# Moving two of sixteen expert weight buffers into the place of layer 1's operands, and re-cutting the others as 10, 2 and 2

## The chip, the core and the metric

The kernel runs on one core of a Trainium2 chip. The metric is the device time of one execution in microseconds, lower is better. The core has a matrix engine (PE, with its weight loads shown as PEld), two engines for element-wise work (DVE and ACT), a general one (POOL) and SP, which in this kernel issues nearly all DMAs. All DMAs that SP issues stand in one queue in order: a DMA whose wait isn't over holds back those behind it.

## The reference, cut to what matters

Two layers of a diffusion backbone over 256 latent and 256 context tokens, width 1024. Each layer has a mixer (an mLSTM head group and an attention head group) and a channel mixer. The second layer's channel mixer is a mixture of 8 experts, of which each latent token uses 2:

```
h = modulate(rms(x));  p = h @ w_in;  y = mixer(p)
x = x + gate1 * (y @ w_out)
layer 0: x = x + gate2 * swiglu(modulate(rms(x)))            # dense
layer 1: top2 = top_k(h @ router, 2)                           # latent tokens alone
         x = x + gate2 * sum_e w_e * (silu(h @ wg[e]) * (h @ wu[e])) @ wd[e]
return rms(x)
```

All is in float32. An expert has three matrices of 1024 x 3584, so the 8 experts bring 352 MB of weights in, and each is read once.

## The kernel before, in words

Up to the experts the kernel works on activations that are kept transposed, features on partitions and 512 tokens in the columns. The operand of every large product is held as a high and a low part (`hh0` to `hh7` and `hl0` to `hl7`, 16 tiles of 128 x 512, made at L319 and listed in `hp`). `gemm` (L342) runs over 128-column units of a weight stream: `Stream` loads a piece (`raw`, L140), ACT and DVE split it into `wh` and `wl` (L149, L150), and three matmuls (L335 to L337) make one product. `mixer` (L388) runs the input projection (`projections`, L766) woven with the mLSTM heads, the attention and the modulation products `adas` (L234), whose weights come as `araw` (L206), two buffers for each step. When the last unit of the input projection is done, the finished heads are written back into `hp` by `split` (L551), in layer 1 into its latent columns 256 to 511 alone. `project` (L796) multiplies them with `w_out`.

The expert weights are taken in the order in which the experts use them: for each expert 2 halves of 8 gate tiles (`in_mg`) and 8 up tiles (`in_mu`) of 896 KB, and then 14 down tiles (`in_md`) of 1024 KB, 46 tiles for an expert and 368 in all. `Ahead` (L931) is their loader. It keeps a ring of `sum(NRW)` = 16 buffers `rawe` of 8 KB a partition. `issue(upto)` issues loads until `upto` of them are out, and `done(left)` issues the next ones for the buffers that the products have just given back. So tile number 16 goes to the buffer of tile 0 and waits for the matmuls that read tile 0.

The ring stands in two pools. `RW` (L929) has 8 buffers and lies where the mixer's tiles lay, so it opens when the mixer of layer 1 is over. `RX` (L1014) has 8 and lies where the weight stream's tiles and `hp` lay (the pools `PW` and `PA`), so it opens when the last product of `project` has read them. `loader.issue(NRW[0])` at L970 issues the first 8 loads and `loader.issue(sum(NRW))` at L1015 the other 8.

Behind `project` come the router (logits L1004, ranks L1081 to L1085), the gathering of the first expert's tokens (L1115) and `experts` (L1159). There the tokens of an expert stand in groups of 32 (`GROUPS`): two groups always, a third behind a branch (L1169) if the expert has more than 64 tokens. `up` (L1177) is run for gate and up, in two steps of 4 tiles each (`UPS`), each step over all groups, so 4 buffers come free only when the last group of a step is done with them. `down` is like it with its own steps (`DOWNS`); L1185 is the up matmul and L1215 the down matmul. `turn` (L1231) transposes the hidden values (`hT`, L1237). A scheduler orders the instructions of each engine when the kernel is built.

Of the kernel before, what the change touches and what calls it, by code (L numbers as in the profile page):

```python
# [9 lines left out]
F32 = mybir.dt.float32  # L10
F32R = mybir.dt.float32r
# [8 lines left out]
KT = 8  # L20
TOK = 512
CTX = 256
# [20 lines left out]
SC = 448  # L43

STEPS = (((0, 1, 56, 30), (7.5, 3.2, 2.2, 4.6)), ((0, 1, 45, 20), (6, 2.2, 2.2, 4.6)))
NRW = (8, 8)


UNITS = ["g", "k0", "k1", "q0", "q1", "v0", "v1", "v2", "v3",
# [6 lines left out]
TAILD = 3  # L56
# [18 lines left out]
def tile_hybrid(ctx: ExitStack, tc, a, tap=None):  # L75
# [23 lines left out]
    def run(g):  # L99
        for _ in g:  # L100
            pass

    def step(g, n=1):
        for _ in range(n):
            next(g, None)

    def upto(g, mark):
        for m in g:
            if m == mark:
                return  # L110


    p1, pa, pw = ExitStack(), ExitStack(), ExitStack()
    P1 = p1.enter_context(tc.tile_pool(name="p1", bufs=1, side="right", reuse_waits="tile"))
    PA = pa.enter_context(tc.tile_pool(name="pa", bufs=1, side="right", reuse_waits="tile"))
    PW = pw.enter_context(tc.tile_pool(name="pw", bufs=1, side="right", reuse_waits="tile"))
# [14 lines left out]
    class Stream:  # L131


        def __init__(self, src):
            self.src, self.raw, self.w, self.ahead = src, [], [], 0
# [112 lines left out]
    def mod(layer, i, j):  # L248

        return mods[layer, i // 2][:, (i % 2) * 8:(i % 2) * 8 + 8, j]  # L250
# [10 lines left out]
    def new_acc():  # L261
        return P1.tile([128, TOK], F32, tag="acc", name="acc", bufs=1)
# [45 lines left out]
    def coef(layer, which):  # L308
        w = (n1, n2)[which]
        A = new_coef()  # L310
        for j in range(2):
            if which and layer == 1 and j == 1:
                continue
            dve.scalar_tensor_tensor(A[:, :, j], mod(layer, 3 * which + 1, j), 1.0, w[:, layer, :],
                                     op0=ALU.add, op1=ALU.mult)
        return A


    hp = [(PW.tile([128, TOK], F32R, name=f"hh{k}"), PW.tile([128, TOK], F32R, name=f"hl{k}")) for k in range(KT)]  # L319

    def modulated(A, b, layer, which, halves, ks=range(KT)):

# [18 lines left out]
    def gemm(units, rhs, evac, nk, head=0, halves=False, tail=0):  # L341

        units = list(units)
        n = len(units)
        b0 = base[0]
        base[0] += n * nk
        o = {}

        def product(u, k, c0, c1):
            lo = max(units[u][0], c0)
            if lo >= c1:
                return
            i = k * head + u if u < head else u * nk + k
            wh, wl = stream.tile(b0 + i)
            mm3(o[u][:, lo:c1], wh, wl, rhs[k][0][:, lo:c1], rhs[k][1][:, lo:c1], k == 0, k == nk - 1)

        cuts = [c[:2] for c in HALVES]
        if head:  # L360
            for u in range(head):
                o[u] = ps("mm", name="mm")
            for c0, c1 in cuts if halves else [(0, TOK)]:
                for k in range(nk):
                    for u in range(head):
                        product(u, k, c0, c1)
                        if k == nk - 1 and c1 == TOK:
                            evac(units[u][1], o[u], units[u][0], c1)
                    yield
        for u in range(head, n - tail):  # L370
            o[u] = ps("mm", name="mm")
            for k in range(nk):
                product(u, k, 0, TOK)
            evac(units[u][1], o[u], units[u][0], TOK)
            yield
        if tail:
            yield "tail"
            for u in range(n - tail, n):
                o[u] = ps("mm", name="mm")
            for c0, c1 in cuts:  # L380
                for u in range(n - tail, n):
                    for k in range(nk):
                        product(u, k, c0, c1)
                    evac(units[u][1], o[u], c0, c1)
                    yield


    def mixer(layer, pool, extra):  # L388


        full = layer == 0
# [3 lines left out]
        def units(keys):  # L395
            for k in keys:
                yield q0 if k[0] in "qo" or k in ("a0", "a1", "a2", "a3") else 0, k
# [23 lines left out]
        for h in range(4):  # L421
            z = 64 * (1 - h % 2)
            nc.gpsimd.memset(kz[h][z:z + 64, :], 0.0)
        for h in range(2):
            z = 64 * (1 - h)
# [7 lines left out]
        def flush():  # L433
            while pend:
                f, key = pend.pop(0)
                f()
                ready.add(key)
# [328 lines left out]
        def projections(keys):  # L766

            yield from gemm(units(keys), hp, evac, KT)
            flush()
            done.append(True)  # L770

        def at():
            while not set(qa_keys) <= ready:
                yield
            yield from qk_norm()
            for j in range(4):
                yield from attend(j)
# [24 lines left out]
    def bridge(p, tail, acc, layer, which, g):  # L802

        upto(p, "tail")
        A = coef(layer, which)
        S = Stats(acc[0])
        nxt = base[0] // 8
        step(p, tail)
        stream.ensure(nxt)
        step(p)  # L810
        S.sums(0, CTX)
        stream.ensure(nxt + 1)
        step(p)
        b = S.spread(0, CTX)
        modulated(A, b, layer, which, HALVES[:1], range(0, 3))
        run(p)
        stream.ensure(nxt + 2)
        modulated(A, b, layer, which, HALVES[:1], range(3, 6))
        step(g, 3)
        S.sums(CTX, TOK)  # L820
        modulated(A, b, layer, which, HALVES[:1], range(6, 8))
        step(g, 3)
        S.spread(CTX, TOK)
        modulated(A, b, layer, which, HALVES[1:], range(0, 4))
        step(g, 2)
        modulated(A, b, layer, which, HALVES[1:], range(4, 8))
# [37 lines left out]
    a0, mx = ExitStack(), ExitStack()  # L864
# [22 lines left out]
    S.sums(0, TOK)  # L887
    M0 = mixer_pool("mix0", a0)
    g = mixer(0, M0, adas(lambda: mx.pool, (0, 1), (0, 2), (1, 0)))
    A = new_coef()  # L890
    def products0(k):
        o = ps("ax", name="ada")
        products(o, k, 0, True, True)
        return o

    z = products0(0)
    b = S.spread(0, TOK)
    stream.ensure(0)
    for k in range(KT):
        row = z  # L900
        if k + 1 < KT:
            z = products0(k + 1)
# [15 lines left out]
    p = project(0, 0, acc)  # L918
    acc2 = []
    g = ffn(acc2)  # L920
    bridge(p, TAIL, acc, 0, 1, g)

    p, g = g, mixer(1, mixer_pool("mix1"), adas(lambda: mx.pool, (1, 1), (1, 2)))
    bridge(p, TAILD, acc2, 1, 0, g)
    run(g)
    mx.close()


    RW = ctx.enter_context(tc.tile_pool(name="rw", bufs=1, reuse_waits="tile"))  # L929

    class Ahead:  # L931

# [8 lines left out]
        def issue(self, upto):  # L941
            while len(self.t) < min(upto, len(self.src)):
                i = len(self.t) % sum(NRW)
                pool, n = (RW, NRW[0]) if i < NRW[0] else (RX, NRW[1])
                t = pool.tile([128, 2048], F32, tag="raw", name="rawe", bufs=n)
                src, c = self.src[len(self.t)]
                nc.sync.dma_start(t[:, 0:c], src())
                self.t.append(t)
# [7 lines left out]
        def done(self, left):  # L956

            self.issue(self.n - left + sum(NRW))

    def weights(e):  # L960

        return (lambda w, st, k: a[("mg", "mu")[w]][bass.ds(e(), 1), st, k].squeeze(0),
                lambda c: a["md"][bass.ds(e(), 1), c].squeeze(0))


    turn_of = []
    loader = Ahead([weights(lambda: 0)] + [weights(lambda p=p: turn_of[p - 1]) for p in range(1, NE)])
    acc = [new_acc()]
    p = project(1, CTX, acc)
    loader.issue(NRW[0])  # L970
    wr0 = P1.tile([128, KT, NE], F32, name="wr0")
    nc.gpsimd.dma_start(wr0, a["router"])
    step(p, HEAD)

    g2 = RW.tile([128, D], F32, name="g2")
    g2c = mod(1, 5, 0)
    for c in range(2):
        o = ps("ax", name="g2p")
        for q in range(4):
            k = 4 * c + q  # L980
            pe.matmul(o[:, q * 128:(q + 1) * 128], g2c[:, k:k + 1].to_broadcast([128, 128]), ident,
                      start=True, stop=True)
        act.activation(g2[:, c * 512:(c + 1) * 512], o, AF.Copy)
    zb = RW.tile([128, 512], BF, name="zb")
    nc.gpsimd.memset(zb, 0.0)


    scale, shift = (RW.tile([128, KT], F32, name=n) for n in ("scale", "shift"))
    dve.scalar_tensor_tensor(scale, mod(1, 4, 0), 1.0, n2[:, 1, :], op0=ALU.add, op1=ALU.mult)
# [5 lines left out]
    for k in range(KT):  # L995
        pe.matmul(o[:, 0:NE], shift[:, k:k + 1].to_broadcast([128, 128]), wr0[:, k, :], start=(k == 0), stop=(k == KT - 1))
    lc = RW.tile([128, NE], F32, name="lc")
    act.activation(lc, o[:, 0:NE], AF.Copy)
# [15 lines left out]
    RX = ctx.enter_context(tc.tile_pool(name="rx", bufs=1, reuse_waits="tile"))  # L1014
    loader.issue(sum(NRW))  # L1015
    RS = ctx.enter_context(tc.tile_pool(name="rs", bufs=1, reuse_waits="tile"))
# [23 lines left out]
    with tc.issue_after(behind_lg):  # L1040
        for t in range(2):
            for c in range(2):
                s = slice(c * 512, (c + 1) * 512)
                p = ps("ax", name="xT")
# [260 lines left out]
    with tc.issue_after(behind_oh[0]), tc.issue_after(behind_th):  # L1305
# [4 lines left out]
        rows = lambda v: v.unsqueeze(1).to_broadcast([128, NE, NE])  # L1310
        cols = lambda v: v.unsqueeze(2).to_broadcast([128, NE, NE])
# [211 lines left out]
```

## Time and profile before

| what | us |
|---|---|
| median of 3 runs (lowest, highest) | 1774.93 (1770.13, 1779.02) |
| the profiled execution, its own time | 1775.88 |
| its span in the profile | 1774.1 |
| PE busy in the span | 1713.3 (97%) |
| DVE busy, ACT busy | 600.1, 448.6 |

The profile's span begins with the first instruction and ends with the last one; the execution's own time has 1.8 us around it. Read in 40 slices, PE is busy at nine tenths or more in nearly all of them at the full granted clock. The DMA engines are at two to eight tenths in the first 20 slices; from slice 22 on they move about 419 GB/s, with lower slices of 406, 391 and 338 GB/s (26 to 28) and 160 GB/s in the last.

### The profile page before, as it was taken

To read this page: it belongs to the slowest core of one execution; us is meant where nothing else is said; L and a number is where in the kernel's file an instruction comes from. 1 tells how busy PE (TensorE), PEld (TensorE's weight loads), DVE (VectorE), ACT (ScalarE), POOL (GpSimd) and SP (SyncE) were. 2 spreads that over 40 slices of the span, in tenths; PEclk is the share of its full clock that TensorE was granted. 3 is DMA by queue.
4 is the path that set the end of the run, shared out by engine and by line. 5 is a ranking of instruction groups with operands and counts; after the bars stand their busy time and mean duration, and the time that the engine had idled before them with its cause. 6 is when DMAs were issued, how large, how long until landed. Compare 5 with 4: busy or idle time off the path is not lost. (4 is left out here: it accounts for less than half of the span.)

```text
span 1774.1 us, 31022 instructions
## 1 busy us (share of the span) xinstructions
PE 1713.3 (97%) x13032; PEld 997.4 (56%) x13032; DVE 600.1 (34%) x1400; ACT 448.6 (25%) x863; POOL 19.4 (1%) x42
## 2 busy tenths in 40 slices
PE   6999999999999999998999999999999999999995
PEld 4865457988888889875764433433333343333432
DVE  6734665733333336647531200201212021210213
ACT  4543553422223323545430100100100010100101
POOL 1000000000000000000000000000000000000000
PEclk9999999999999999999999999999999999999997
DMA  8435552232332222365589999998999999999993
GB/s 323 154 107 190 174 180 63 84 95 97 97 104 95 96 96 95 119 198 188 190 357 418 419 419 419 406 391 338 417 419 418 419 404 418 419 418 420 416 418 160
DMA packets 84860, 472.68 MB, mean 266 GB/s; under 512 B 9424, under 2 KB 9808, under 8 KB 69088
## 3 DMA queue, kind: packets, MB, share of 16 engines
q1 hardware_dynamic: 84240, 469.36, 68.0%
q8 instruction: 117, 1.92, 0.4%
q0 software_dynamic: 176, 0.56, 0.1%
q10 hardware_dynamic: 288, 0.52, 0.1%
q14 instruction: 39, 0.32, 0.0%
HBM read 469.36 MB, written 1.05 MB: 265 GB/s over the span
## 5 line engine op out<-in xcount | busy, mean ns | idle before, releaser
L1185 PE MATMUL up<-rawe,G 128*32 128x448 f32 x5120 | 507.2, 540 | 3.7 <-PEq L1169 2.6
L1185 PEld LDWEIGHTS up<-rawe,G 128*32 128x32 f32 x5120 | 184.3, 110 | 301.0 <-issue 280.4
L335 PE MATMUL mm<-hh,wh 128*128 128x512 f32 (+1 forms) x856 | 305.5, 360 | 3.4 <-ACT hh L330 3.4
L336 PE MATMUL mm<-hl,wh 128*128 128x512 f32 (+1 forms) x856 | 304.5, 356 | 0.0
L337 PE MATMUL mm<-hh,wl 128*128 128x512 f32 (+1 forms) x856 | 303.5, 355 | 0.0
L1215 PE MATMUL y<-rawe,e 128*32 128x512 f32 x2240 | 263.7, 593 | 1.8 <-PEq L1169 1.2
L149 ACT ACTIVATE wh<-raw 128x1024 fp32r<-128x1024 f32 x120 | 127.1, 1059 | 326.3 <-PE mm L336 290.7
L150 DVE TENSOR_TENSOR wl<-raw,wh 128x1024 fp32r<-128x1024 f32 x120 | 146.7, 1223 | 176.4 <-ACT wh L149 173.8
L335 PEld LDWEIGHTS mm<-hh,wh 128*128 128x128 f32 x856 | 161.0, 189 | 30.8 <-issue 4.8
L336 PEld LDWEIGHTS mm<-hl,wh 128*128 128x128 f32 x856 | 161.8, 189 | 27.3 <-issue 5.2
L337 PEld LDWEIGHTS mm<-hh,wl 128*128 128x128 f32 x856 | 161.7, 189 | 23.6 <-issue 1.6
L1215 PEld LDWEIGHTS y<-rawe,e 128*32 128x32 f32 x2240 | 78.3, 110 | 160.9 <-issue 155.4
L1238 ACT ACTIVATE e<-hT 128x384 f32<-128x384 f32 x48 | 22.7, 491 | 418.6 <-PE hT L1237 418.6
L1257 DVE TENSOR_TENSOR hid<-sg,up 128x448 f32<-128x448 f32 x48 | 27.0, 617 | 241.8 <-PE up L1185 241.8
L335 PE MATMUL mm<-fh,wh 128*128 128x512 f32 (+1 forms) x209 | 74.5, 356 | 0.0
L336 PE MATMUL mm<-fl,wh 128*128 128x512 f32 (+1 forms) x209 | 74.3, 355 | 0.0
L337 PE MATMUL mm<-fh,wl 128*128 128x512 f32 (+1 forms) x209 | 74.3, 355 | 0.0
L1239 DVE COPY e<-hT 64x128 f32<-64x128 f32 x48 | 13.6, 284 | 163.3 <-ACT e L1238 163.2
L214 PE MATMUL ada<-araw,cz 128*32 128x256 f32 x640 | 54.3, 390 | 13.4 <-DMA araw<-in_ada_dram 13.4
L1154 DVE SCALAR_TENSOR_TENSOR xt<-scat,wet,xt 128x512 f32<-128x512 f32 x32 | 22.6, 746 | 117.4 <-PE scat L1153 117.3
L1140 DVE TENSOR_TENSOR ye<-y,yc 32x512 f32<-32x512 f32 x48 | 32.7, 682 | 73.9 <-ACT yc L1138 73.2
L1253 ACT ACTIVATE sg<-up 128x448 f32<-128x448 f32 x48 | 22.9, 544 | 124.0 <-PE up L1185 124.0
(292 smaller groups left out, 1389.9 us busy)
## 6 DMA issues: line engine op xcount, KB each, us to landing
rawe<-in_mg_dram SPq DMA_DIRECT2D x128, 896.0 KB, 17.4
rawe<-in_mu_dram SPq DMA_DIRECT2D x128, 896.0 KB, 16.2
rawe<-in_md_dram SPq DMA_DIRECT2D x112, 1024.0 KB, 19.1
raw<-in_ws_dram SPq DMA_DIRECT2D x120, 512.0 KB, 3.5
araw<-in_ada_dram SPq DMA_DIRECT2D x80, 512.0 KB, 4.6
a<-in_ada_dram SPq DMA_DIRECT2D x8, 1024.0 KB, 11.2
xall<-in_xT_dram SPq DMA_DIRECT2D x2, 1024.0 KB, 6.3
fn<-in_fn_dram POOLq DMA_DIRECT2D x1, 512.0 KB, 8.8
```

The source lines that it names most:

```text
L149: act.activation(h, raw, AF.Copy)
L150: dve.tensor_sub(l, raw, h)
L214: pe.matmul(o[32 * g:32 * g + 32, 0:256], cz[:, kt, 16 - 2 * row:48 - 2 * row], t[:, z:z + 256], start=(first and kt < 4), stop=(last and ...
L335: pe.matmul(out, wh, hh, start=first, stop=False)
L336: pe.matmul(out, wh, hl, start=False, stop=False)
L337: pe.matmul(out, wl, hh, start=False, stop=last)
L1140: dve.tensor_add(ye[32 * s:32 * s + 32, n * 512:(n + 1) * 512], y[s][32 * n:32 * n + 32, :], yc[32 * n:32 * n + 32, :])
L1185: last = pe.matmul(o[s][32 * c:32 * c + 32, 0:SC], g[:, k, 32 * s:32 * s + 32], w[k][:, c * SC:(c + 1) * SC], start=(k == 0), stop=(k == K ...
L1215: last = pe.matmul(y[s][r:r + 32, :], e[s][:, 2 * i + par, :], w[i][:, par * 1024 + n * 512:par * 1024 + (n + 1) * 512], start=(i == 0), s ...
L1238: act.activation(e[s][:, 12 * st:12 * st + 12, :], pt[:, 0:384].rearrange("p (q c) -> p q c", c=32), AF.Copy)
L1253: act.activation(sg[s], o[:, 0:SC], AF.Silu)
L1257: dve.tensor_mul(hid[st, s], sg[s], o[:, 0:SC])
```

## The change

The tuple of ring sizes becomes four numbers. The 16 operand tiles become four of 8 KB a partition, `hp0` to `hp3`, in a pool `PH` of their own that stays open to the end. In layer 1, when the input projection is done, `hp` is rebuilt from two tiles of the latent columns alone (`hp0` and `hp1` again, read through `Late`, which shifts the columns), and the places of `hp2` and `hp3` take expert tiles 0 and 1, whose loads are issued there. Expert tiles 2 to 11 stand in the mixer's place, 12 and 13 in the places of `hp0` and `hp1` when `project` has read them, 14 and 15 in the weight stream's place. The ring still has 16 buffers.

```diff
-NRW = (8, 8)
+NRW = (2, 10, 2, 2)
+    PH = ctx.enter_context(tc.tile_pool(name="ph", bufs=1, side="right", reuse_waits="tile"))
...
-    hp = [(PW.tile([128, TOK], F32R, name=f"hh{k}"), PW.tile([128, TOK], F32R, name=f"hl{k}")) for k in range(KT)]
+    def parts(n, cols):
+        per = 2048 // cols
+        z = [PH.tile([128, per, cols], F32R, tag=f"hp{i}", name=f"hp{i}", bufs=1) for i in range(n)]
+        z = [z[i // per][:, i % per, :] for i in range(2 * KT)]
+        return list(zip(z[0::2], z[1::2]))
+    class Late:
+        def __init__(self, t):
+            self.t = t
+        def __getitem__(self, at):
+            rows, cols = at
+            return self.t[rows, cols.start - CTX:TOK - CTX if cols.stop is None else cols.stop - CTX]
+    hp = parts(4, TOK)
...
             yield from gemm(units(keys), hp, evac, KT)
             flush()
             done.append(True)
+            if not full:
+                hp[:] = [tuple(Late(z) for z in y) for y in parts(2, CTX)]
+                loader.issue(NRW[0])
...
-                pool, n = (RW, NRW[0]) if i < NRW[0] else (RX, NRW[1])
-                t = pool.tile([128, 2048], F32, tag="raw", name="rawe", bufs=n)
+                pool, tag, n = [(lambda: PH, "hp2", 1), (lambda: PH, "hp3", 1), *[(lambda: RW, "raw", NRW[1])] * NRW[1], (lambda: PH, "hp0", 1),
+                                (lambda: PH, "hp1", 1), *[(lambda: RX, "raw", NRW[3])] * NRW[3]][i]
+                t = pool().tile([128, 2048], F32, tag=tag, name="rawe", bufs=n)
...
-    loader.issue(NRW[0])
+    loader.issue(NRW[0] + NRW[1])
```

The loader itself is now made ahead of layer 1's mixer, since it issues from inside it. Two places in SP's queue move, and one on PE.

In SP's queue between layer 1's mixer and the routing, the order before is this (`raw` is the stream's weights, `araw` the modulation's, `rawe` an expert tile, `number` the experts' order):

```order
L206 DMA araw<-in_ada_dram 128x1024 x4
L140 DMA raw<-in_ws_dram 128x1024
L206 DMA araw<-in_ada_dram 128x1024 x12
L140 DMA raw<-in_ws_dram 128x1024
L947 DMA rawe<-in_mg_dram 128x1792 x8
L947 DMA rawe<-in_mu_dram 128x1792 x5
L1169 UNCONDITIONAL_BRANCH x2
L947 DMA rawe<-in_mu_dram 128x1792 x3
L1351 TENSOR_LOAD number
```

and the same stretch of the changed kernel, whose lines have moved down by 3 to 26:

```order
L209 DMA araw<-in_ada_dram 128x1024 x2
L967 DMA rawe<-in_mg_dram 128x1792 x2
L209 DMA araw<-in_ada_dram 128x1024 x2
L143 DMA raw<-in_ws_dram 128x1024
L209 DMA araw<-in_ada_dram 128x1024 x12
L143 DMA raw<-in_ws_dram 128x1024
L967 DMA rawe<-in_mg_dram 128x1792 x6
L967 DMA rawe<-in_mu_dram 128x1792 x7
L1195 UNCONDITIONAL_BRANCH x2
L967 DMA rawe<-in_mu_dram 128x1792
L1377 TENSOR_LOAD number
```

Two of the sixteen first loads now stand in the middle of a run of four `araw` loads; the other fourteen follow the last `raw` as the sixteen did before.

On PE the instructions and their waits are the same up to the second half of the first expert. There the order before is this (`hT` is a transpose of hidden values, `up` a matmul of an expert tile, the branch guards the third group):

```order
L1185 MATMUL up<-rawe,G 32x448 x27
L1237 MATMUL hT<-sml,hid 128x128 x3
L1237 MATMUL hT<-sml,hid 64x128
L1237 MATMUL hT<-sml,hid 128x128 x3
L1237 MATMUL hT<-sml,hid 64x128
L1185 MATMUL up<-rawe,G 32x448
L1237 MATMUL hT<-sml,hid 128x128 x3
L1237 MATMUL hT<-sml,hid 64x128
L1185 MATMUL up<-rawe,G 32x448 x20
L1169 COMPARE_AND_BRANCH
L1185 MATMUL up<-rawe,G 32x448 x16
L1169 UNCONDITIONAL_BRANCH x2
```

and in the changed kernel this:

```order
L1211 MATMUL up<-rawe,G 32x448 x31
L1263 MATMUL hT<-sml,hid 128x128 x3
L1263 MATMUL hT<-sml,hid 64x128
L1195 COMPARE_AND_BRANCH
L1211 MATMUL up<-rawe,G 32x448 x16
L1195 UNCONDITIONAL_BRANCH x2
L1263 MATMUL hT<-sml,hid 128x128 x3
L1263 MATMUL hT<-sml,hid 64x128
L1211 MATMUL up<-rawe,G 32x448
L1263 MATMUL hT<-sml,hid 128x128 x3
L1263 MATMUL hT<-sml,hid 64x128
L1211 MATMUL up<-rawe,G 32x448 x43
```

The branch with its 16 matmuls has moved from behind the three groups of transposes to between the first and the second. The number of matmuls is the same.

## Rows read from the trace of the kernel before

**Rows 1.** Busy time by stretch: engines (instructions), granted clock, DMA share, GB/s.

```profile
874.00:896.00 22.00, 22.00 (x187) 20.51 (x186) 8.14 (x17) 6.05 (x12) 0.53 (x1) 1.00 0.97 391
896.00:900.00 4.00, 4.00 (x37) 3.58 (x35) 1.24 (x3) 0.42 (x1) 0.00 (x0) 1.00 0.12 48
900.00:915.00 15.00, 14.23 (x108) 9.01 (x105) 11.48 (x68) 10.25 (x18) 0.58 (x1) 1.00 0.95 372
915.00:918.00 3.00, 2.79 (x33) 0.98 (x29) 1.07 (x8) 0.32 (x1) 0.00 (x0) 1.00 1.01 419
1200.00:1240.00 40.00, 40.00 (x352) 15.32 (x348) 4.03 (x13) 3.15 (x7) 0.00 (x0) 1.00 0.82 333
1700.00:1741.00 41.00, 40.34 (x375) 14.25 (x377) 3.39 (x9) 4.25 (x9) 0.00 (x0) 1.00 1.01 418
1741.00:1750.00 9.00, 8.38 (x74) 3.18 (x66) 0.15 (x1) 0.59 (x1) 0.00 (x0) 1.00 0.36 147
```

**Rows 2.** SP's issues in order of time, 850 to 1130 us: start, length, what.

```profile
874.30 4.00 SPq L947 DMA_DIRECT2D rawe<-in_mg_dram  x8
879.82 23.34 SPq L947 DMA_DIRECT2D rawe<-in_mu_dram  x8
918.23 8.80 SPq L947 DMA_DIRECT2D rawe<-in_mg_dram  x8
```

**Rows 3.** SP's waits from 882 to 925 us: total, times, longest.

```profile
SPq L947 <- PE mm L337: 12.6, 1, 12.6
SPq L947 <- PE up L1185: 7.7, 6, 3.4
```

**Rows 4.** PE in order of time, 895 to 935 us.

```profile
899.56 1.26 PE L1004 MATMUL lg<-xall,wr 128*32 128x256 f32 x8
...
912.41 1.31 PE L1185 MATMUL up<-rawe,G 128*32 128x448 f32 x9
...
915.74 10.73 PE L1185 MATMUL up<-rawe,G 128*32 128x448 f32 x112 [0.20 <-PEq L1169]
```

**Rows 5.** Waits of PEld and PE from 912 us on for expert tiles.

```profile
PEld up L1185 <- DMA rawe<-in_mg_dram: 3.2, 7, 1.0
PEld up L1185 <- DMA rawe<-in_mu_dram: 3.1, 8, 0.9
PE up L1185 <- DMA rawe<-in_mu_dram: 0.6, 2, 0.4
PE up L1185 <- DMA rawe<-in_mg_dram: 0.2, 1, 0.2
```

**Rows 6.** SP's waits from 1200 to 1240 us.

```profile
SPq L947 <- PE y L1215: 33.9, 10, 10.6
```

**Rows 7.** DMA issues: count, size of each, median us to landing.

```profile
rawe<-in_mg_dram SPq DMA_DIRECT2D x128, 896.0 KB, 17.4
raw<-in_ws_dram SPq DMA_DIRECT2D x120, 512.0 KB, 3.5
araw<-in_ada_dram SPq DMA_DIRECT2D x80, 512.0 KB, 4.6
```

**Rows 8.** SP's issues around the end of layer 1's input projection.

```profile
810.76 0.33 SPq L206 DMA_DIRECT2D araw<-in_ada_dram  x1
...
819.88 1.73 SPq L206 DMA_DIRECT2D araw<-in_ada_dram  x2
```

**Rows 9.** PE there: the projection's last matmul, the next modulation products.

```profile
811.23 0.28 PE L337 MATMUL mm<-hh,wl 128*128 128x256 f32 x1
...
819.18 1.07 PE L214 MATMUL ada<-araw,cz 128*32 128x256 f32 x16
```

**Rows 10.** Busy time by stretch there, columns as in the first group.

```profile
812.00:815.00 3.00, 3.00 (x13) 1.84 (x13) 2.71 (x7) 2.99 (x8) 0.82 (x2) 1.00 0.46 168
815.00:820.00 5.00, 4.20 (x32) 2.42 (x30) 4.66 (x16) 2.93 (x8) 1.23 (x2) 1.00 0.01 2
```

**Rows 11.** PEld in the first expert's transposes, idle before each in brackets.

```profile
945.19 0.83 PEld L1237 LDWEIGHTS hT<-sml,hid 128*128 128x128 f32 x8 [0.73 <-issue]
...
947.09 0.39 PEld L1237 LDWEIGHTS hT<-sml,hid 128*128 128x128 f32 x4 [0.73 <-DVE e L1239]
```

More of the change, by code (lines that the diff above doesn't have):

```diff
@@ L923, in tile_hybrid @@
     p, g = g, mixer(1, mixer_pool("mix1"), adas(lambda: mx.pool, (1, 1), (1, 2)))
[L924 to L929, printed above, removed]
     class Ahead:
@@ L967, in tile_hybrid @@
     loader = Ahead([weights(lambda: 0)] + [weights(lambda p=p: turn_of[p - 1]) for p in range(1, NE)])
+    bridge(p, TAILD, acc2, 1, 0, g)
+    run(g)
+    mx.close()
+    RW = ctx.enter_context(tc.tile_pool(name="rw", bufs=1, reuse_waits="tile"))
     acc = [new_acc()]
     p = project(1, CTX, acc)
-    loader.issue(NRW[0])
+    loader.issue(NRW[0] + NRW[1])
     wr0 = P1.tile([128, KT, NE], F32, name="wr0")
```

## The prediction, made before the changed kernel ran

> **What bounds the kernel now.** I read the stretches first, then SP's queue, since the change moves only DMAs, and then PE around the moment at which the experts start.
>
> The experts take almost half of the span. In the stretches the reader is to see two things full at once: PE is busy in nearly all of each stretch, and the DMA engines move 418 or 419 GB/s in the steady ones [rows 1]. Both can't be the limit everywhere, so I ask who waits for whom. From the first expert matmul at 912.41 us [rows 4] PE's matmuls and weight loads wait for expert tiles for 3.2 + 3.1 + 0.6 + 0.2 = 7.1 us in all, no wait longer than 1.0 us [rows 5]. The pace agrees: 112 up matmuls in 10.73 us [rows 4] are 0.38 us for four that run side by side, with no gap between fours. SP on its side waits for PE: from 1200 to 1240 us 33.9 us go into waiting for down products to give buffers back [rows 6], and the DMA share falls to 0.82 there [rows 1]; all 16 buffers are full and the DMA engines have nowhere to write. So PE's chain of expert products from 912.41 us sets the end, and the DMA engines keep up with it with about 7 us lost.
>
> Ahead of the experts the DMA engines do have holes: after 9 tiles (8 loads at 874.30 us and one at 879.82 us [rows 2]) SP waits 12.6 us for the last matmuls of the output projection [rows 3], and from 896 to 900 us only 48 GB/s move [rows 1]. The other seven tiles follow up to 903.2 us (879.82 + 23.34) [rows 2]. The change fills that hole and another one in the mixer. What it is worth depends on what happens at 918.23 us, where the 17th load is issued [rows 2]: the queue waits there for PE's up matmuls, 7.7 us over six waits, the longest 3.4 [rows 3], because that load goes to the buffer of tile 0, which is in use until both groups have passed the first four tiles.
>
> **The change part by part.**
>
> *Two loads earlier, at the end of layer 1's input projection.* A tile is 896 KB [rows 7], 0.918 MB, and takes 0.918 / 0.419 = 2.19 us at the steady rate; two take 4.4 us. They wait for the projection's last matmul, at 811.23 + 0.28 = 811.5 us [rows 9], and stand behind the `araw` load issued at 810.76 us [rows 8], which is 0.52 MB or 1.25 us. So they are in at about 817.5 us. The `araw` loads behind them wait for the products that start at 819.18 us and are issued at 819.88 us [rows 8, 9]; from 815 to 820 us the DMA engines are idle, share 0.01 [rows 10]. That idle time is the cover: cost 0, with 2.4 us to spare. Without it an `araw` pair would come up to 4.4 us late, and PE with it. Below zero there is nothing, as no work waits for the pair before 912 us. I take 0.
>
> *Ten loads instead of eight when the mixer's place comes free.* Same issue time, 874.30 us, and the same wait ahead of it. With the last `raw` piece (0.52 MB) they are 9.70 MB, 23.1 us, and keep the engines full up to about 898 us. No `raw` piece is left to be delayed; the one beside them is first in the queue. Cost on the path 0.
>
> *Four loads instead of seven behind the projection.* From about 899.6 us, when the matmuls give way to the logits [rows 4], four tiles take 8.8 us and are in at 908.4 us. Before, seven took 15.3 us and were in by about 918 us, with 419 GB/s still moving from 915 to 918 us [rows 1]. So the sixteenth tile lands 9.6 us earlier.
>
> *What this is worth.* The start of the experts doesn't need it. Between 899.56 us and 912.41 us PE runs the routing and the gathering of tokens [rows 4], and these depend on no expert tile. The first expert's gate tiles are 0 to 7, in since 896 us both ways; its first up tile is wanted after 8 gate tiles in two groups, 16 steps of two fours of 0.38 us each, 12 us after the start, at 924 us, when all 16 tiles are in both ways. The 17th load still waits for PE at 918.23 us. So from 918 us on the two kernels are in the same state: 16 tiles landed, none in flight, the same ring of 16 and the same order. What the change gains is turned into a longer idle time of the DMA engines, 908 to 918 us. Bounds: 0 on one side; on the other 7.1 us, all of PE's waits for expert tiles [rows 5], if every one of them came from a ring that was late from the start. The stall at 1200 us speaks for 0: there the ring is full, so whatever lead the loads had is cut off. I take 0.
>
> *Operands in four tiles, and the latent halves in two.* The matmuls, splits and modulations keep their number, shape, order and, on PE, their waits up to the middle of the first expert; one split in layer 1 waits for four more matmuls of the projection, at most 4 x 0.28 us [rows 9], off PE's path. Cost 0, bounds 0 and 1.1 us.
>
> *The order in the first expert.* The branch moves in between the transposes. Around these PEld has two gaps of 0.73 us [rows 11]; one branch or matmul more in between can close them or add one of the same size, so the bounds are -1.5 and +1.5 us. As one branch and three groups stand there both ways, I take 0.
>
> **The sum.** The profiled execution took 1775.88 us, 1774.1 us of span and 1.8 us around it. With 0 for every part the changed kernel's like is 1775.9 us. That profile lies 0.95 us above the median of the three runs, 1774.93 us, so the median to expect is 1774.9 us.
>
> The page "DMA: Bandwidth & Descriptors" of the Trainium skill (Rules for kernel authors) advises to issue a DMA early, compute, and wait on it late; read as a promise for this change it gives the first rival below. No run here has shown it yet, and the row at 918.23 us speaks against it, because the early loads don't make the next one early.
>
> **The rivals.**
>
> *The early loads carry through (faster).* If the ring's lead at 918 us counted, up to 9.6 us of loading would be saved, of which PE could use its 7.1 us of waits: 1774.9 - 7.1 = 1767.8 us. For it: the DMA engines are full in nearly every stretch from 900 to 1741 us [rows 1]. Against it: SP waits for PE at 918.23 us [rows 3], and again at 1200 us [rows 6]. It decides only if the 17th load no longer had to wait for PE, and the ring is not longer than it was. Chance 0.06.
>
> *The early pair blocks the modulation's weights (slower).* SP's queue holds fourteen `araw` loads behind the pair. If the pair were issued later than about 815.5 us (819.88 - 4.4), because the last reader of its place is later than the matmul at 811.23 us, the next `araw` pair would land up to 4.4 us late, PE would wait at its modulation products, and mixer, projection and experts would all follow: 1774.9 + 4.4 = 1779.3 us. For it: PE runs these products as soon as it comes to them, and the place of the pair lies in the order in front of them. Against it: 8 us between the last reader and the next `araw` issue [rows 8, 9]. Chance 0.06.
>
> The same page of the Trainium skill (Queues, rings and completion order) says that descriptors on one engine's ring are consumed in ring order; by that the full 4.4 us would fall on the `araw` loads and not a share of it. The rows here show no such case.
>
> *The early loads aren't early (no change).* If the pair waited for something else of the mixer it would land with the ten at 874 us. Twelve tiles from 874.30 us and four from 899.6 us would then be in at about 910 us, still ahead of 918.23 us. The time is the same, so this shares the forecast's 0.88 with the case that all goes as computed.
>
> **How the numbers follow.** 0.88 for no effect, at 1774.9 us; 0.06 for 1767.8 us; 0.06 for 1779.3 us. The three runs before lie from 1770.1 to 1779.0 us, so a median of the changed kernel may lie some 4 us to either side without any cause. About 0.5%, 8.9 us, is what a measurement of this kernel can tell from no change. Both rivals are smaller than that (-0.4% and +0.25%), so most of their chance falls to "same" too; they pass the bound only together with that scatter. That gives 0.06 faster, 0.89 same, 0.05 slower. For 8 times in 10 the range must hold the scatter and reach to both rivals: 1768 to 1781 us.
>
> **What would show it right or wrong.** In the changed profile two `in_mg` loads are issued at about 811.6 us and the next modulation products start at 819.2 us as before. The stretch 896 to 900 us is full, the one from 909 to 918 us is empty. The first expert matmul stands at 912.4 us and the 17th load at 918.2 us. The dip between 1200 and 1240 us is still there, and the last expert matmul ends at about 1750 us, as in [rows 1]. It is wrong if the first expert matmul moves by more than 2 us, if the modulation products wait for `araw` after 819 us, or if the experts take another time from first to last matmul at the same start.

## The result, and the profile after

The changed kernel takes 1784.89 us (median of 8 runs, 1783.86 to 1790.37) against 1776.12 for the kernel before (8 runs); the ratio is 1.0057, with a 95% interval of 1.0047 to 1.0067. I had forecast no effect and a time up to 1781; it is slower, and by more than my 0.5%. The profiled execution took 1784.85 us, 8.97 more than that of before.

The loads are issued in the forecast order. SP's issues in order of time, of the changed kernel, in answer to [rows 2, 8] (start, length, what):

```profile
819.43 0.90 SPq L967 DMA_DIRECT2D rawe<-in_mg_dram  x2
...
881.85 4.45 SPq L967 DMA_DIRECT2D rawe<-in_mg_dram  x6
886.34 22.30 SPq L967 DMA_DIRECT2D rawe<-in_mu_dram  x8
925.59 9.05 SPq L967 DMA_DIRECT2D rawe<-in_mg_dram  x8
```

and PE in order of time, in answer to [rows 4]:

```profile
906.93 1.27 PE L1030 MATMUL lg<-xall,wr 128*32 128x256 f32 x8
...
919.76 1.31 PE L1211 MATMUL up<-rawe,G 128*32 128x448 f32 x9
...
923.09 10.73 PE L1211 MATMUL up<-rawe,G 128*32 128x448 f32 x112 [0.21 <-PEq L1195]
```

The pair goes out early, and the 17th load goes out 5.83 us after the first expert matmul, as before (918.23 - 912.41 = 5.82). But that matmul comes at 919.76 us and not at 912.41, and everything here is 7.35 us late. Busy time by stretch, columns as in [rows 1], each stretch of before moved by 7.35 us:

```profile
881.35:903.35 22.00, 22.00 (x188) 20.51 (x187) 7.91 (x18) 6.05 (x12) 0.00 (x0) 1.00 0.96 390
903.35:907.35 4.00, 4.00 (x37) 3.59 (x35) 1.22 (x3) 0.42 (x1) 0.00 (x0) 1.00 0.89 321
907.35:922.35 15.00, 14.19 (x107) 9.01 (x105) 11.47 (x68) 10.23 (x18) 0.58 (x1) 1.00 0.70 272
922.35:925.35 3.00, 2.79 (x33) 0.97 (x29) 1.07 (x8) 0.32 (x1) 0.00 (x0) 1.00 0.00 0
1207.35:1247.35 40.00, 40.00 (x352) 15.31 (x348) 4.01 (x13) 3.14 (x7) 0.00 (x0) 1.00 0.84 336
```

The hole between projection and logits is filled (DMA share 0.89 for 0.12), the idle time has moved to just ahead of the 17th load (0.00 for 1.01), PE does the same work in the same time in each stretch, and the dip at 1200 us is still there. So the loss lies ahead of all this. The page's groups of matmuls show it. Of the kernel before (busy us, mean ns of one, behind the bar):

```profile
L335 PE MATMUL mm<-hh,wh 128*128 128x512 f32 (+1 forms) x856 | 305.5, 360 | 3.4 <-ACT hh L330 3.4
L336 PE MATMUL mm<-hl,wh 128*128 128x512 f32 (+1 forms) x856 | 304.5, 356 | 0.0
L337 PE MATMUL mm<-hh,wl 128*128 128x512 f32 (+1 forms) x856 | 303.5, 355 | 0.0
```

and of the changed kernel:

```profile
L355 PE MATMUL mm<-hp,wh 128*128 128x512 f32 (+1 forms) x856 | 308.7, 364 | 4.2 <-ACT hp L350 4.0
L356 PE MATMUL mm<-hp,wh 128*128 128x512 f32 (+1 forms) x856 | 307.7, 360 | 0.1
L357 PE MATMUL mm<-hp,wl 128*128 128x512 f32 (+1 forms) x856 | 306.6, 359 | 0.0
...
L355 PE MATMUL mm<-fh,wh 128*128 128x512 f32 (+1 forms) x209 | 74.5, 356 | 0.0
```

The same 2568 matmuls on these operands (`hh` and `hl` before, `hp` after) are 4 ns longer in the mean, with 0.9 us more waiting in all; those on the feed-forward operand `fh` keep the 356 ns that they have before. Matmuls overlap in the pipeline, so what one costs is the step from start to start. Two stretches full of `mm` matmuls give it, the first on `hp`, the second on `fh` and `fl`. All such stretches from here on count only the instructions that write or read `mm`, on DVE and ACT too. The kernel before (columns: PE, PEld, DVE, ACT, granted clock, DMA share, GB/s):

```profile
400.00:450.00 50.00, 50.00 (x222) 41.42 (x221) 2.77 (x4) 2.91 (x5) 1.00 0.31 99
475.00:515.00 40.00, 40.00 (x178) 33.14 (x177) 5.20 (x12) 0.00 (x0) 1.00 0.31 100
```

and the changed kernel:

```profile
400.00:450.00 50.00, 50.00 (x215) 40.18 (x214) 3.46 (x5) 2.31 (x4) 1.00 0.29 93
475.00:515.00 40.00, 40.00 (x178) 33.10 (x178) 5.24 (x12) 0.00 (x0) 1.00 0.29 94
```

PE is busy for all 50 us in both, at the full granted clock, and yet it starts 222 matmuls in one and 215 in the other. By their start times a 512-column matmul on `hp` takes 226.7 ns before in the steady stretches and 234.3 after; on `fh` it takes 227 in both. Up to the end of layer 0's feed-forward layer, 1485 of them follow each other without a wait, at a mean of 227.4 and 234.2 ns: 10.2 us. 277 matmuls of 256 columns are 1.3 ns shorter: -0.4 us. That is 9.8, and the next matmul there stands at 692.51 us before and 702.35 after: 9.84. Some 2.5 us come back in layer 1, so that PE is 7.35 us late at the experts: between these two points PE waits 5.5 us in all for the modulation's weights (`araw`) before and 2.8 us after. This wait is no fixed size: in a later run with the pace of before (the kernel before with a plain ring) PE waits 3.3 us there and the first expert matmul comes at 909.88 us. So the 7.35 us hold some 2 us of scatter, and the sum over the matmuls, 9.8 us, is the better measure of what the change costs. 1.63 us are lost again at the end, and 7.35 + 1.63 = 8.98 is the whole difference.

The last 1.63 us stand at the last down products. PE in order of time, of the kernel before:

```profile
1741.49 6.06 PE L1215 MATMUL y<-rawe,e 128*32 128x512 f32 x50
1748.09 1.92 PE L1215 MATMUL y<-rawe,e 128*32 128x512 f32 x16 [0.54 <-SPq L1360]
```

and of the changed one:

```profile
1749.68 4.38 PE L1241 MATMUL y<-rawe,e 128*32 128x512 f32 x36
1754.61 1.92 PE L1241 MATMUL y<-rawe,e 128*32 128x512 f32 x16 [0.56 <-SPq L1386]
1757.08 1.92 PE L1241 MATMUL y<-rawe,e 128*32 128x512 f32 x16 [0.54 <-SPq L1386]
```

It breaks off twice, because the last tiles come later. The first and the last expert matmul are 837.01 us apart before and 838.64 after.

### The profile page after: what moved, and what is told of

It is laid out like the page before. It is cut to its first block, busy times and chain, and to the rows that moved or that the text cites. A ratio compares the mean times of both kernels' runs of the same rounds, so it can differ in the third digit from the quotient of the medians.

```text
span 1783.1 us, 31032 instructions
## 1 busy us (share of the span) xinstructions
PE 1722.6 (97%) x13031; PEld 993.7 (56%) x13032; DVE 600.3 (34%) x1400; ACT 448.4 (25%) x863; POOL 19.3 (1%) x42
## 5 line engine op out<-in xcount | busy, mean ns | idle before, releaser
L355 PE MATMUL mm<-hp,wh 128*128 128x512 f32 (+1 forms) x856 | 308.7, 364 | 4.2 <-ACT hp L350 4.0
L356 PE MATMUL mm<-hp,wh 128*128 128x512 f32 (+1 forms) x856 | 307.7, 360 | 0.1
L357 PE MATMUL mm<-hp,wl 128*128 128x512 f32 (+1 forms) x856 | 306.6, 359 | 0.0
L355 PEld LDWEIGHTS mm<-hp,wh 128*128 128x128 f32 x856 | 160.6, 189 | 35.0 <-ACT hp L350 5.4
L356 PEld LDWEIGHTS mm<-hp,wh 128*128 128x128 f32 x856 | 161.4, 189 | 30.6 <-issue 5.2
L357 PEld LDWEIGHTS mm<-hp,wl 128*128 128x128 f32 x856 | 161.3, 188 | 26.9 <-issue 1.6
```

Source lines behind the costliest of these rows:

```text
L355: pe.matmul(out, wh, hh, start=first, stop=False)
L356: pe.matmul(out, wh, hl, start=False, stop=False)
L357: pe.matmul(out, wl, hh, start=False, stop=last)
```

## The experiments

**What could change the pace of a matmul that is itself unchanged.** The change moves the operands in the on-chip memory: in the built programs `hh0` begins at byte 105536 of a partition and `hp0` at 196576, the weights `wh` at 146496 and 113728, `fh` at 18240 in both. My first theories were A, that the start of the moving operand must be a multiple of 64 bytes, whatever the weights' is; C, that the place high in the memory is slow; and B, that the early loads cost the time.

*The changed kernel with operands on a multiple of 64 bytes.*

```diff
+    pad0 = PH.tile([128, 8], F32, name="pad0")
     hp = parts(4, TOK)
+    pad1 = PH.tile([128, 8], F32, name="pad1")
```

> The changed kernel with 32 bytes of padding ahead of the operand tiles hp0 to hp3 and 32 behind them, so that they start at byte 196544 of a partition (a multiple of 64) instead of 196576 (32 past one); all else keeps its place modulo 64. Theory A (a 512-column matmul whose moving operand starts 32 bytes past a multiple of 64 takes 234 ns from start to start instead of 227): back to the kernel before, 1774 to 1779 us, 227 ns, first expert matmul at 912 to 913 us. Theory B (the two early loads cost the time): still 1783 to 1787 us. Theory C (the place at the end of the partition costs it, whatever its alignment): still 1783 to 1787 us and 234 ns.

Measured: 1781.34 us, ratio 1.0034 (1.0022 to 1.0046). The stretches of above:

```profile
400.00:450.00 50.00, 50.00 (x216) 40.41 (x215) 3.46 (x5) 2.32 (x4) 1.00 0.30 94
475.00:515.00 40.00, 40.00 (x177) 32.86 (x176) 5.25 (x12) 0.00 (x0) 1.00 0.31 95
```

Still 216 and not 222: A falls. (B and C had 1783 to 1787 us, which the median misses too.) `fh`, which has not moved, is slower too (229 ns), and what has moved against it are the weights, by 64 bytes.

*The kernel before with operands moved by 32 bytes, weights not; and with the weights moved by 32 and the operands by 64.*

```diff
+    pad0 = PW.tile([128, 8], F32, name="pad0")     # both; ahead of hp in the first, behind it in the second
     hp = [(PW.tile([128, TOK], F32R, name=f"hh{k}"), PW.tile([128, TOK], F32R, name=f"hl{k}")) for k in range(KT)]
+    pad1 = PW.tile([128, 8], F32, name="pad1")     # behind hp in the first, behind late_consts() in the second
```

> The kernel before with its 16 operand tiles 32 bytes past a multiple of 64 (hh0 at byte 105504 instead of 105536), every other tile where it was modulo 64. Theory A: as slow as the changed kernel up to the experts, +6 to +9 us, 1782 to 1786 us, 234 ns for 512 columns. Theories B and C: as before, 1774 to 1779 us, 227 ns.

> The kernel before with the weight stream's tiles raw, wh and wl 32 bytes past a multiple of 64 and the operands hh, hl on one. Theory A (only the moving operand counts, since a weight load lies beside the matmul ahead of it): no change, 1774 to 1779 us. A rival of it (any operand of a matmul off a multiple of 64 costs): +6 to +13 us.

Measured: ratios 1.0051 (1.0034 to 1.0067) and 1.0057 (1.0039 to 1.0076). So the kernel before becomes nearly as slow as the changed one by a pad of 32 bytes (233.3 ns for 234.3), with its operands at the low place and without early loads: C isn't needed, nor is B. A had forecast this first result; for the second it had forecast no change, and it fails again. In the second run the matmuls on `fh` become slower as well, though `fh` stands where it stood:

```profile
400.00:450.00 50.00, 50.00 (x216) 40.25 (x216) 3.46 (x5) 2.33 (x4) 1.00 0.30 95
475.00:515.00 40.00, 40.00 (x173) 32.15 (x172) 4.38 (x10) 0.00 (x0) 1.00 0.33 97
```

*The changed kernel without the early call of the loader.* `loader.issue(NRW[0])` was taken out of the mixer.

> The changed kernel without the two early issues: tiles 0 and 1 are issued with the ten at the end of the mixer, all places in memory as in the changed kernel. Theory A: as slow as the changed kernel, 1783 to 1787 us, since the operands lie where they lay. Theory B: back to 1774 to 1779 us.

Measured: 1.0067 (1.0048 to 1.0087). This experiment failed: the scheduler still puts the two loads in front of the modulation's, and SP issues them at 819.10 us. It repeats the changed kernel and says nothing on B; the last run below does.

**The difference between the two places.** Theory R: what counts is the start of the moving operand less that of the weights, modulo 128 or 256 bytes. It is 0 in the kernel before and 160 in the changed one. (In the three expectations that follow, B is another theory, that both starts count by themselves.) First the cost by itself:

```diff
+    for n, step in ((2, 1), (1, 27)):
+        for c in range(64):
+            m, w = divmod(c * step % 64, 8)
+            for cols in (512, 256):
+                for _ in range(n):
+                    group(8 * m, 8 * w, cols)
```

> This kernel computes nothing of the reference: it runs only chains of 24 float32r matmuls like those of the projections and the feed-forward layer (eight steps of three: weight 1 on operand 1, weight 1 on operand 2, weight 2 on operand 1), 512 and 256 columns wide, with no DMA beside them. The start of the moving operand goes through the eight multiples of 32 bytes within 256, and that of the weights too: 64 pairs, each visited twice in different orders, with 48 and then 24 matmuls of each width; the output is zeros. Theory R (relative): a 512-column matmul takes 226.7 ns from start to start where the moving operand and the weights have the same offset modulo 128 or 256 bytes, 229 to 234 ns elsewhere; so the diagonal of the table is fast. Theory B (both absolute): fast only where both stand at 64 (or 64 and 192); about 4 cells of 64 at 227 ns and the rest at 233. Theory P (phase): the pace is set by the moment at which a chain starts, not by addresses; the two visits to the same pair then differ by 4 ns or more in many cells. Theory C (the place at the high end of SBUF): no cell is slow, since the operand stands at 24.7 KB here. For 256 columns I expect 113 to 120 ns, the slowest where both stand at 64.

Measured, mean ns from start to start on the first visit, for 512 columns; rows are the operand's start modulo 256, columns the weights':

```
           0     32     64     96    128    160    192    224
    0  227.2  233.2  233.4  234.3  232.2  233.4  229.1  233.2
   64  229.1  233.2  227.2  233.2  233.2  234.1  232.1  233.4
  160  234.3  232.1  233.4  229.1  233.2  227.2  233.2  233.4
  224  233.2  233.4  234.3  232.1  233.3  229.1  233.3  227.2
```

The four rows left out repeat the pattern, shifted: to within 2 ns the pace of 512 columns depends on the difference alone, modulo 256 and not 128. The second visit differs by at most 1.6 ns, where P had 4 or more, so P falls; all eight pairs with difference 0 are fast, where B had about four fast pairs in all, so B falls. The view by stretch of this kernel shows three cells, at a difference of 0, 192 and 160 (of the `mm` matmuls alone; columns: PE, PEld, clock, DMA share, GB/s):

```profile
24.50:34.50 10.00, 10.00 (x46) 8.28 (x45) 1.00 0.01 2
125.50:135.50 10.00, 10.00 (x45) 8.23 (x44) 1.00 0.00 0
696.60:706.60 10.00, 10.00 (x44) 8.05 (x43) 1.00 0.01 2
```

There is no DMA to speak of beside them, so no other traffic is needed. The map gives back what the kernels had shown (means, ns):

| kernel, operand | difference | in the kernel | in the map |
|---|---|---|---|
| before, hp / fh | 0 / 0 | 227.4 / 226.7 | 227.3 |
| changed, hp | 160 | 234.2 | 234.3 |
| on a multiple of 64, hp / fh | 192 / 64 | 233.3 / 228.9 | 233.3 / 229.1 |
| before with 32 bytes, hp | 224 | 233.3 | 233.2 |
| before with weights moved, hp / fh | 224 / 32 | 233.3 / 233.3 | 233.2 / 233.2 |

Then the change with the difference put right: two small tiles, 160 bytes with their padding, change places with the operands, and the start is 64 modulo 256 as that of the weights.

```diff
+    hp = parts(4, TOK)                                     # ahead of the constants
-    ones = P1.tile([128, 1], F32, name="ones")
+    ones = PH.tile([128, 1], F32, name="ones")
+    mod12 = PH.tile([128, 16, 2], F32, name="mod12")       # used for layer 1, part 2
```

> The changed kernel with its operands moved down by 160 bytes, so that they start 64 bytes above a multiple of 256 as the weights and the feed-forward operands do (two small constant tiles, 32 and 128 bytes, change places with them; nothing else is changed). Theory R and theory B: 512-column matmuls on the operands fall from 234.3 to 226.7 ns, the first expert matmul comes at about 912 us and not 919.8, and the ratio to the kernel before is 1.001 (only the 1.6 us at the end of the ring stay; 1777 us). Theory C: the operands still stand at 196 KB, so 234 ns and a ratio of 1.0057. Theory P: anything from 226.7 to 234.

and the kernel before with operands and weights moved together (`pad1` alone):

> The kernel before with one pad of 32 bytes above everything in the weights' pool, so that projection operands and weights move down together, from 64 to 32 bytes above a multiple of 256; the feed-forward operands stay at 64. Theory R: the matmuls on hh and hl keep 226.7 ns and only those on fh and fl go to 233.4 (some 430 of them, +2.8 us): ratio 1.0016, 1779 us. Theory B: all of them go to 233.4 ns, +11 to +14 us, ratio about 1.007, as in the run with both shifted by different amounts. Theory C: nothing moves, ratio 1.000.

Measured: 1.0011 (1.0001 to 1.0021), the first expert matmul at 912.80 us; and 1.0016 (1.0007 to 1.0025). The changed kernel with the right difference, with its operands still at the high place:

```profile
400.00:450.00 50.00, 50.00 (x222) 41.42 (x221) 2.77 (x4) 2.91 (x5) 1.00 0.33 99
475.00:515.00 40.00, 40.00 (x178) 33.14 (x177) 5.00 (x12) 0.00 (x0) 1.00 0.32 98
```

and the kernel before, moved as a whole:

```profile
400.00:450.00 50.00, 50.00 (x222) 41.41 (x221) 2.77 (x4) 2.90 (x5) 1.00 0.34 101
475.00:515.00 40.00, 40.00 (x173) 32.13 (x172) 4.38 (x10) 0.00 (x0) 1.00 0.31 92
```

Both as theory R has it: 222 again in each, and in the second only the matmuls on `fh` fall, to 173, since it is now 32 bytes off. In the changed kernel with the right difference the matmul behind layer 0's feed-forward layer stands at 692.72 us (692.51 before, 702.35 in the changed kernel). This settles the 9.8 us and with them the late start of the experts, and C is out.

*Is there a better difference than 0?* The same kind of chain, 0 to 252 bytes in steps of 4, and pairs in which the two operands or the two weights differ:

```diff
+    for c in range(64):
+        for cols in (512, 256):
+            for _ in range(2):
+                group(cols, c, c, 0, 0)
```

> Like the map of 64 pairs, this kernel computes nothing of the reference and has zeros for output: chains of 24 float32r matmuls with no DMA beside them. First part: the moving operand starts 0, 4, 8, ... 252 bytes above the weights (modulo 256), 512 and 256 columns wide. Second part: the two moving operands of a step stand at different offsets, each at the eight multiples of 32 bytes. Third part: the two weights stand at different offsets. Theory R in its plain form (the pace depends on the difference alone, and 0 is the best for 512 columns): no cell of 512 columns is below 226.5 ns, and those at differences that are no multiple of 32 lie between their neighbours, 227 to 235; for 256 columns the best is 113.5. Rival R2 (a collision between the stream of the operand and the loading of the next weights, which some other distance avoids altogether): somewhere a cell is near 512 / 2.4 = 213 ns, or at 220, and then a version of this kernel with that distance would be up to 2100 x 6.7 ns = 14 us faster than the kernel before.

Measured: 226.7 ns at 0 is the lowest of all cells for 512 columns; 4 bytes off is 238.2, the highest about 240. Where the two operands or the two weights of a step differ, no cell is below 227 either. R2 falls, and so does R's clause that steps of 4 lie between their neighbours.

**The 1.6 us at the end.** Load 150 goes out 326.68 us after the first expert matmul before, and 328.3 to 328.4 us in the four kernels with the changed ring. Such a lag comes and goes along the ring (load 170 goes out at 363.06 and 363.04 us); what counts is that it is there at the last load, at 815.83 us before and 817.26 to 817.53 in those four. In the built programs load 150 waits for PE's count 6110 before and 6118 after. Within a pool of several buffers a load is given the one that was released first, so pools of 8 and 8 and of 1, 1, 10, 1, 1 and 2 hand out different buffers. A tag for each buffer makes it a plain ring. On the changed kernel with the right difference, and on the kernel before:

```diff
-*[(lambda: RW, "raw", NRW[1])] * NRW[1]
+*[(lambda: RW, f"raw{j}", 1) for j in range(NRW[1])]       # RX likewise; the kernel before likewise
```

> The changed kernel with its operands at the weights' offset (as in the run before) and with one more edit: each of the 16 buffers of the ring has a tag of its own, so that load i always goes to buffer i modulo 16; with pools of several buffers the load takes whichever of the pool was released first. Theory L (the lag of 1.6 us at the end comes from which buffer a load is given): load 150 waits for PE's count 6110 again and not 6118, the time from the first to the last expert matmul falls from 838.36 to 837.0 us, ratio to the kernel before 1.000 (1775.5 us). Rival M (the lag comes from the start of the ring, where the 17th load finds an empty queue): it stays at 838.4 us, ratio 1.001.

> The kernel before with that edit alone: 16 buffers with a tag each. Many loads wait for an earlier product of PE than before (load 44 for count 4708, not 4712), none for a later one. Theory L: the loads come up to 1 us earlier, and the experts take 837.0 us or up to 1 us less; ratio 0.9995 to 1.000. Rival M: 837.0 us, nothing changes.

Measured: 0.9992 (0.9981 to 1.0004) and 0.9998 (0.9985 to 1.0011). SP's waits from 1200 to 1250 us, of the changed kernel, in answer to [rows 6]:

```profile
SPq L967 <- PE y L1241: 35.3, 10, 12.4
```

and of the one with the right difference and the plain ring:

```profile
SPq L968 <- PE y L1242: 36.2, 14, 10.7
```

The longest wait is 10.7 us again, as the 10.6 of before; load 150 goes out at 326.63 us and the last load at 815.50, and from the first to the last expert matmul it is 836.60 us (838.36 without the plain ring, 836.58 in the kernel before with one). M falls. The whole change, put right in two places, is not slower than the kernel before, and not faster either.

*A version that might beat both.* For 256 columns the map had its best pace at 192, 113.6 ns against 119.9 at 0. With the plain ring, layer 1's latent halves were written 64 bytes lower:

```diff
+            return self.t[rows, cols.start - 16:(TOK if cols.stop is None else cols.stop) - 16]
```

> The kernel before with the fixed ring, and the latent halves of layer 1's operands for the output projection written 64 bytes lower, over columns that nobody reads any more: these 192 matmuls of 256 columns then stand 192 bytes from the weights (modulo 256). Theory R with the map of 64 pairs: they take 113.6 ns and not 120, 192 x 6.4 = 1.2 us less ahead of the routing, first expert matmul at about 911.2 us; ratio 0.999. If the pace of 256 columns at that distance is not settled (the second map had 117.8 there): 0.4 us less, ratio 0.9995.

Measured: 0.9993 (0.9979 to 1.0006). The 192 matmuls take 113.8 ns, as the map has it, and the last one starts 32.08 us after the first, for 33.12 in the kernel before with a plain ring. But a gain of 1 us is less than the time of the whole kernel can tell.

*The early pair, truly undone*: the operands stay in all four tiles, so no load can stand in front of the modulation's.

```diff
-            if not full:
-                hp[:] = [tuple(Late(z) for z in y) for y in parts(2, CTX)]
-                loader.issue(NRW[0])
```

> The run of the changed kernel with operands at the weights' offset and a fixed ring, without its early part: layer 1's operands stay in all four tiles until the output projection has read them, so no expert tile can be loaded in front of the modulation's weights; ten tiles go when the mixer is over and six behind the projection. Theory E0 (my prediction's: the early loads are worth nothing, the 17th load waits for PE in any case): the 17th load is issued 5.8 us after the first expert matmul as before, the experts take 836.6 us as with the pair, first expert matmul within the 2 us by which it scatters from run to run; ratio to the kernel before 0.999 to 1.000. Theory E+ (the early pair carries through): the experts take up to 4.4 us longer without it (two tiles of 2.19 us), ratio up to 1.002. Theory B (the early pair costs the mixer time): the first expert matmul comes up to 4.4 us earlier than with the pair, ratio down to 0.997.

Measured: 1.0001 (0.9988 to 1.0015), against 0.9992 (0.9981 to 1.0004) with the pair; the intervals overlap. SP's issues:

```profile
808.31 13.91 SPq L218 DMA_DIRECT2D araw<-in_ada_dram  x4
...
874.35 5.52 SPq L964 DMA_DIRECT2D rawe<-in_mg_dram  x8
881.98 20.14 SPq L964 DMA_DIRECT2D rawe<-in_mu_dram  x8
918.28 6.34 SPq L964 DMA_DIRECT2D rawe<-in_mg_dram  x5
```

The first expert matmul stands at 912.46 us (911.92 with the pair), the 17th load 5.82 us behind it, load 150 at 326.69 us. The experts take 837.79 us, 1.2 more than with the pair, which arises only behind load 170. Neither E0 (836.6) nor the 4.4 us of E+ is hit. The other seven kernels with the ring of before or a plain one take 836.43 to 837.01 us, so 1.2 us would be much for scatter; whether it is the pair's doing stays open. The theory that the pair costs the mixer time (B at first) falls: without it the experts don't start earlier.

## Why the prediction was wrong

*Two loads earlier, at the end of layer 1's input projection*, and the ten and the four loads: right in what they do to the 17th load and the experts, wrong in some sizes. The pair runs in the idle time that I had found, and the stretches that answer to [rows 10], moved by 8.5 us (PE is 8.3 us late there), show it:

```profile
820.50:823.50 3.00, 3.00 (x13) 1.88 (x12) 2.75 (x6) 2.97 (x8) 0.82 (x2) 1.00 0.88 302
823.50:828.50 5.00, 4.20 (x32) 2.28 (x29) 4.66 (x15) 3.03 (x8) 1.48 (x3) 1.00 0.68 280
```

The DMA engines are now at 0.68 where they were at 0.01, and PE is busy for 4.20 us in both. The next modulation weights go out at 828.18 us, 8.30 later than before [rows 8], so the pair doesn't hold them back. But the 2.4 us to spare weren't there: the pair is issued at 819.43 us and its second tile lands at 828.22, just as the next weights go out. *What this is worth*: right up to the 17th load. The sixteenth tile lands 1.96 us after the first expert matmul against 7.72 before, so 5.8 us earlier and not 9.6; the 17th, which waits for PE, lands 10.19 us after it against 10.18. There the lead ends, as forecast, and the early pair is worth between nothing and 1.2 us.

*Operands in four tiles, and the latent halves in two*: this is the step that failed. I wrote that the matmuls "keep their number, shape, order and, on PE, their waits" and priced it at 0, with bounds of 0 and 1.1 us. Number, shape and order did stay the same, and so did the waits but for 0.9 us; yet each matmul of 512 columns took 234.3 ns in the steady stretches and not 226.7, because the move changed how the operands stand to the weights. I had treated the place of a tile as if it had no price. That was an assumption and stood in no row, and my bounds covered only waits. It cost 9.8 us up to the end of the feed-forward layer, of which 7.35 are left at the experts, from which all of *the experts in the same state* started late.

"The same ring of 16 and the same order" is the second miss, a smaller one. The order is the same, but with other pools a load is given another buffer and waits for another product: 1.6 us. Two of the prediction's own signs of being wrong came true: the first expert matmul moved by more than 2 us, and the experts took another time.

*The order in the first expert*: 0, as forecast. The gaps of [rows 11] are the same, by PEld's rows there,

```profile
952.55 0.39 PEld L1263 LDWEIGHTS hT<-sml,hid 128*128 128x128 f32 x4 [0.73 <-issue]
...
954.78 0.39 PEld L1263 LDWEIGHTS hT<-sml,hid 128*128 128x128 f32 x4 [0.73 <-DVE e L1265]
```

and load 44, behind it, goes out 56.84 us after the first expert matmul against 56.68.

The two rivals with a price were wrong as well. Neither touched the matmuls of layer 0, and the slower one, at 1779.3 us, rested on late modulation weights: PE waited less for them than before, 2.8 us for 5.5.

## What to carry to other kernels

When an edit moves tiles, list what reads them at full rate, and ask what the new place costs, even if every instruction, wait and shape is the same: here a difference of 160 bytes (modulo 256) between operand and weights cost 9.8 us in some 1500 matmuls. Count the instructions in a stretch of 100% busy time before and after; the busy share alone is 100% in the slow kernel too. And a ring cut into other pools is another ring: compare for which instruction each load waits, and not only the order.

## What the runs showed of the hardware

- A float32r matmul of 512 columns with 128 x 128 weights takes 227 ns from start to start (544 cycles at 2.4 GHz, granted clock 1.00) when operand and weights have the same start modulo 256 bytes. At other multiples of 32 it takes 229 (difference 64), 232 or 233 (128), 233 (32, 96, 192, 224) or 234 ns (160), and between them from 229 to about 240 ns. Why, no run here shows. The Trainium skill says on its page "SBUF — State Buffer" (Who interferes with whom) that PE never waits on another engine. The map agrees as far as it goes: no other engine worked beside its chains (DMA share at most 0.01 in the three stretches), and what changed the pace from 227 to 234 ns was the place of PE's own two inputs.
- With 256 columns it is the other way round: of the multiples of 32, 0 is among the slowest (119.8 ns), as are 96 and 128; 64 and 192 are the fastest, though there the pace is now 113.5 and now 117.8 ns from chain to chain.
- The place in the memory, low or high, made no difference to either: at the low place of before and at the high one of the changed kernel with the right difference it is 226.7 ns for 512 columns and 120 ns for 256.
